# A planner's numbers changed in a float32 hybrid-attention layer: loads' consumers listed later behind their transfers, equal slack for float32 steps

## The chip, the cores and the metric

The kernel runs on one core of a Trainium2 chip. The core has five engines that run side by side, each through its own list of instructions in order: TensorE (PE, matmuls and transposes), VectorE (DVE), ScalarE (ACT), GpSimd (POOL) and SyncE (SP), which here issues nearly all transfers between the chip's memory (DRAM) and the core's buffers. An instruction that waits holds everything listed behind it on its engine. The metric is the device time of one execution in microseconds (us); of several runs the median is given.

## The reference

One layer over 2048 tokens of width 1024, all in float32:

```python
xn = rms_norm(x, mix_norm_g)
aq, ak, av, mq, mk, mv, mo, ipre, fpre, ga, gm = split(xn @ w_in)
att = chunk_band_attention(aq, ak, av, rel_bias)        # 8 heads of 64, own chunk of 64 tokens and 8 before
mq, mk = split(silu(causal_depthwise_conv([mq, mk])))
hm = rms_norm_per_head(mlstm_chunkwise(mq, mk, mv, ipre, fpre))   # 4 heads of 128, chunkwise recurrence
y = sigmoid(ga) * (att @ w_att_proj) + sigmoid(gm) * (sigmoid(mo) * hm @ w_mlstm_proj)
x = x + y @ w_out
x = x + square(relu(rms_norm(x, ffn_norm_g) @ w_up)) @ w_down     # inner width 4096
return rms_norm(x, final_norm_g)
```

## The kernel before, in words

The tokens are four blocks of 512; a tile is 128 partitions by 512 columns. A float32 product is made of three faster ones in the format float32r: each operand is split into a high part (rounded on ACT, a `copy` into float32r) and a low part (`tensor_sub` on DVE, the operand minus its high part), and `mm3` adds high*high, high*low and low*high in a PSUM bank. Such pairs of parts lie in the tiles `r` (activations) and `wsp` (weights). Matmuls of this kind are L631, L662, L667, L562 to L564 and L856 in the profile.

The large products use a seven-product scheme on 2 x 2 blocks instead of eight products. So sums and differences of blocks are formed on DVE (L1765, L1855, L520, L438), spilled to DRAM by `store` (L2043), and loaded back later. The stages follow each other: the first input projections (`quad`, L631), the far ones (`in_far`, `product`, L662 and L667) with the token mixers of blocks 0 and 1 between them, the output projection and the up projection of blocks 0 and 1, their down projection (`down`, L562 to L564) with the mixers of blocks 2 and 3 between, and the same again for blocks 2 and 3. The mixers are attention (`scores` L1337, `turn` L1369, `weigh` L1262) and recurrence (`rec_head`, L1586 to L1651).

What sets the order is a planner, `Flow`, that runs on the host when the kernel is built. Every piece of work is a generator ("thread") that yields an engine and an expected time, for example `yield "act", act_ns(512)`; for a transfer, `yield "sp", 800, 2000` says that the queue is held for 800 ns and the data are there 2000 ns after that. The planner keeps a clock for each engine and always takes the thread whose step can start first. Nothing of this is executed on the chip: the times only decide in what order instructions are listed; what an instruction waits for on the chip are semaphores. Behind the planner the framework's own list scheduler may still move instructions within some microseconds of plan time.

Three of the planner's rules matter here.

- A step on PE gets extra time before it counts as ready: `FAR` for float32r work, `SLACK` for a step that works in full float32 and so switches PE over (marked `"pe~"`: transposes L1369, L1651, L1586, the recurrence's products L1597, L1612 to L1616), and `NEAR` when PE is already in full float32.
- `fl.put(pool, tile, late=...)` gives a tile back to its pool as of a later time, so that its next writer is listed later.
- A load's third number is how long behind its queue time the consumer is listed. `take_u1` (L2101) loads a spilled operand into an `r` tile and then rounds it, L1109 on ACT and L1114 on DVE; it serves the far input projections (from `xu`), the mixers' results (from `mix`) and the down projections (from `u`). `square_kept` (L2070) loads a tile to square it (L2075, L2079). The gate load in `rec_head` is L1648.

`store` (L2042) yields the queue, issues the transfer, sets its event at once and gives the tile back to its pool. `kept_row` (L1715) loads such a spilled tile again; its rounding, with a factor, is L1111 on ACT and L1116 on DVE. L780 is the evacuation of a bank in `park_v` and `finish_far`; L501 and L503 split a weight tile.

Loads into operand tiles go through a ring: 16 tiles in the far projections and in the second down projection, 8 in the first one (`N_RING = (8, 16)`). The tiles named below are `r` (operand parts), `wsp` and `wraw` (split and raw weights), `tmp`, `ctx` (512-column scratch), `sc` (scores), `bank` (PSUM).

Of the kernel before, what the change touches and what calls it, by code (L numbers as in the profile page):

```python
# [101 lines left out]
class Flow:  # L102
# [3 lines left out]

    SLACK, FAR = 720.0, 1300.0
    NEAR = 150.0  # L110
    SWITCH = 85.0
    LAT = dict(pe=dict(act=190.0, dve=190.0, pool=190.0),
# [2 lines left out]
               sp=dict())  # L115
# [114 lines left out]
def act_ns(n, ps=False, ap=0):  # L230
    return (51 if ps else 93) + 0.834 * n + 93 * ap


def dve_ns(n):
    return 70 + 1.042 * n
# [10 lines left out]


class Layer:
    LATE = 4000.0

    def __init__(self, tc, pool, psum, io):
        self.tc, self.nc, self.io = tc, tc.nc, io
# [197 lines left out]
    def split_w(self, i, src, raw, sent=None):  # L450
        if i == 0:
            yield from self.split_first(src, raw, sent)
            self.fl.put(self.wraw, raw, late=self.LATE)
            return
# [4 lines left out]
        yield from self.split_now(i, raw)  # L459
        self.fl.put(self.wraw, raw, late=self.LATE)  # L460

    def split_turned(self, i, srcs, raw):
# [3 lines left out]
        yield from self.split_now(i, raw)  # L466
        self.fl.put(self.wraw, raw, late=self.LATE)

# [38 lines left out]
    def quad_w(self, i, q, kept, raws, evs):  # L507
# [10 lines left out]
        def sub(n, dst, x, y):  # L518
            yield "dve", dve_ns(1024)
            V.tensor_sub(dst, x, y)  # L520
            if kept:
                fl.spawn(keep(n, dst), 1)
            else:
                fl.set(spilt[n])
# [16 lines left out]
        yield from sub(2, b, d, b)  # L541
        fl.put(self.wraw, d, late=self.LATE)
        yield "wait", [spilt[1]]
        yield from sub(3, a, c, a)
        fl.put(self.wraw, c, late=self.LATE)
        yield from self.split_now(i + 5, b)
        yield "wait", [spilt[2]]
        fl.put(self.wraw, b, late=self.LATE)
        yield from self.split_now(i + 6, a)
# [1020 lines left out]
    def rec_head(self, b, h, r):  # L1570
# [72 lines left out]
        fl.put(self.hs, hs)  # L1643
        (og,) = yield "get", self.temp, 1
        yield "wait", [self.m_ev[b, 2 * MH + h]]
        yield "sp", 800, 2000
        nc.sync.dma_start(og[:, :512], self.mfar[b].ap()[2 * MH + h])
        (bk,) = yield "get", self.banks, 1  # L1648
        yield "pe~", 107 * NT
# [391 lines left out]
    def store(self, dst, src, ev, pool=None, item=None, queue="sp"):  # L2041
        yield queue, 800, 2000  # L2042
        self.nc.sync.dma_start(dst, src)  # L2043
        self.fl.set(ev)
        if pool is not None:
            self.fl.put(pool, item)

    def norm_mid(self, s, h):

# [19 lines left out]

    def square_kept(self, src, j, x, tot, summed, scale=1.0):  # L2070
        x5 = x[0][:, :512]
        yield "sp", 800, 2000
        self.nc.sync.dma_start(x5, src)
        yield "act", act_ns(512)
        self.nc.scalar.activation(tot if j == 0 else x5, x5, AF.Square, scale=scale)  # L2075
        if j > 0:
            yield "wait", [summed[j - 1]]
            yield "dve", dve_ns(512)
            self.nc.vector.tensor_add(tot, tot, x5)  # L2079
        self.fl.put(self.sc, x)  # L2080
        self.fl.set(summed[j])
# [17 lines left out]
        fl.put(self.rpool, *(yield "get", ring, N_RING[s]))  # L2099

    def take_u1(self, src, r, ev):  # L2101
        yield "sp", 800, 2000
        self.nc.sync.dma_start(r[:, 1].bitcast(F32), src)
        yield from self.split(r[:, 1].bitcast(F32), r)
        self.fl.set(ev)
# [458 lines left out]
```

## Time and profile before

| what | value |
|---|---|
| runs shown | 2749.84, 2750.84 and 2754.76 us, median 2750.84 |
| profiled execution, its own time | 2753.07 us |
| its span, first to last instruction | 2751.3 us |
| granted TensorE clock | 0.998 |
| busy share of the span | PE 99%, weight loads 82%, DVE 76%, ACT 55%, POOL 2% |
| transfers | 673.57 MB, 244 GB/s over the span |

A page of the profile gives busy time by engine and by group of instructions. The timeline gives instructions in order of time: start, duration, engine, line, operation, tiles written and read, and in brackets how long the engine had been idle before and what ended that. The list of waits sums this idle time by who waited for whom: total, number of times, longest. A matmul's end is modelled in the trace, so a matmul's row is longer than the distance to the next one.

### The profile page before, as it was taken

Reading aid. Unit: us, or ns where it says so; the run is one execution under the profiler, and the core shown is the slowest. Engines: PE = TensorE matmul, PEld = TensorE weight load, DVE = VectorE, ACT = ScalarE, POOL = GpSimd, SP = SyncE. Lnnn points to the kernel's source line nnn. Section 1 sums busy time; section 2 is a strip of 40 time slices with the busy share of each in tenths; the row PEclk is TensorE's granted clock in tenths of the full one; section 3 lists DMA queues with packets and bytes.
Section 4 is the critical chain, followed back from the end, with each engine's and each line's share of the span. In section 5 each row is a group of like instructions: output and inputs, shape, how many; then the busy total and the mean of one; then the engine's idle time right before and its main releaser. Section 6 shows DMA issues by size and latency. Waiting matters only on the chain.

```text
span 2751.3 us, 38074 instructions
## 1 busy us (share of the span) xinstructions
PE 2724.6 (99%) x12832; PEld 2261.5 (82%) x12832; DVE 2086.0 (76%) x3689; ACT 1526.4 (55%) x2640; POOL 44.6 (2%) x79
## 2 busy tenths in 40 slices
PE   9999999999999999999999999999999999999998
PEld 8878888788888887888888888888888888888887
DVE  7878776888775778897768889888888665667675
ACT  6545446666652434566556766657345565554443
POOL 0000000000000000000000000000000000000000
PEclk9999999999999999999999999999999999999999
DMA  8877678878877888767668778776864454588863
GB/s 295 284 254 268 234 267 281 260 235 266 255 256 254 299 305 294 244 212 260 246 237 295 254 231 223 239 257 199 294 227 171 151 205 154 180 278 281 283 230 137
DMA packets 331992, 673.57 MB, mean 245 GB/s; under 512 B 36900, under 2 KB 66468, under 8 KB 331796
## 3 DMA queue, kind: packets, MB, share of 16 engines
q1 hardware_dynamic: 331076, 670.08, 72.3%
q8 instruction: 101, 1.65, 0.2%
q10 hardware_dynamic: 720, 1.06, 0.1%
q14 instruction: 95, 0.78, 0.1%
HBM read 458.79 MB, written 212.21 MB: 244 GB/s over the span
## 4 chain that ended last, share of the span: by engine, by line
PE 83%; DVE 7%; DMA 4%; issue 3%; ACT 2%; POOL 0%; SPq 0%; POOLq 0%; DVEq 0%; ACTq 0%
PE bank L631 35%; PE bank L662 9%; PE bank L562 9%; PE bank L564 8%; PE bank L563 8%; PE bank L667 2%; PE bank L1337 2%; PE bank L1262 2%; PE bank L1369 2%; DVE wsp L503 1%; PE bank L856 1%; DVE r L1114 1%; DMA yp<-tmp 1%; DMA r<-u 1%; DVE ctx L1765 1%
## 5 line engine op out<-in xcount | busy, mean ns | idle before, releaser
L631 PE MATMUL bank<-r,wsp 128*128 128x512 f32 x4872 | 1110.9, 390 | 4.2 <-ACT r L1109 1.4
L631 PEld LDWEIGHTS bank<-r,wsp 128*128 128x128 f32 x4872 | 912.5, 188 | 198.2 <-ACT r L1109 2.1
L501 ACT CAST wsp<-wraw 128x1024 fp32r<-128x1024 f32 x439 | 461.3, 1051 | 492.1 <-PE bank L631 183.3
L503 DVE TENSOR_TENSOR wsp<-wraw,wsp 128x1024 fp32r<-128x1024 f32 x439 | 537.0, 1223 | 247.0 <-ACT wsp L501 236.7
L562 PE MATMUL bank<-r,wsp 128*128 128x512 f32 x1088 | 429.9, 396 | 0.3 <-DVE scs L1343 0.3
L564 PE MATMUL bank<-r,wsp 128*128 128x512 f32 x1088 | 425.3, 391 | 0.0
L563 PE MATMUL bank<-r,wsp 128*128 128x512 f32 x1088 | 425.2, 391 | 0.0
L662 PE MATMUL bank<-r,wsp 128*128 128x512 f32 x1512 | 370.8, 394 | 3.1 <-DVE ctx L780 2.5
L662 PEld LDWEIGHTS bank<-r,wsp 128*128 128x128 f32 x1512 | 279.4, 189 | 59.4 <-issue 2.7
L564 PEld LDWEIGHTS bank<-r,wsp 128*128 128x128 f32 x1088 | 204.3, 188 | 43.0
L562 PEld LDWEIGHTS bank<-r,wsp 128*128 128x128 f32 x1088 | 204.5, 188 | 38.4 <-DVE scs L1343 0.7
L563 PEld LDWEIGHTS bank<-r,wsp 128*128 128x128 f32 x1088 | 204.7, 188 | 38.1
L1114 DVE TENSOR_TENSOR r<-r 128x512 fp32r<-128x512 f32 x273 | 181.8, 687 | 56.8 <-ACT r L1109 55.0
L1109 ACT CAST r<-r 128x512 fp32r<-128x512 f32 x273 | 164.7, 621 | 104.4 <-DMA r<-u 77.1
L1798 DVE TENSOR_TENSOR ctx<-bank,ctx 128x512 f32<-128x512 f32 x150 | 103.0, 687 | 64.7 <-PE bank L631 63.6
L520 DVE TENSOR_TENSOR wraw<-wraw,wraw 128x1024 f32<-128x1024 f32 x112 | 136.5, 1220 | 2.2 <-DMA wsum<-wraw 1.0
L1350 ACT ACTIVATE sc<-sc,scs 128x640 f32<-128x640 f32 (+4 forms) x128 | 97.2, 760 | 54.9 <-DVE scs L1343 54.3
L1790 ACT COPY ctx<-bank 128x512 f32<-128x512 f32 x150 | 87.2, 581 | 52.0 <-PE bank L631 50.5
L2119 ACT ACTIVATE ctx<-ctx 128x512 f32<-128x512 f32 x96 | 60.5, 630 | 97.8 <-DVE ctx L1798 97.8
L1374 DVE TENSOR_TENSOR r<-bank,r 128x512 fp32r<-128x512 f32 (+1 forms) x168 | 96.4, 595 | 8.4 <-ACT r L1372 7.5
L1262 PE MATMUL bank<-r,r 128*128 128x512 f32 x336 | 95.7, 367 | 3.5 <-DVE ctx L1674 1.9
L1372 ACT CAST r<-bank 128x512 fp32r<-128x512 f32 (+1 forms) x168 | 80.7, 514 | 27.9 <-PE bank L1369 27.4
(257 smaller groups left out, 3054.1 us busy)
## 6 DMA issues: line engine op xcount, KB each, us to landing
wraw<-in_wf SPq DMA_DIRECT2D x196, 512.0 KB, 4.2
r<-u SPq DMA_DIRECT2D x224, 256.0 KB, 4.4
wraw<-wsum SPq DMA_DIRECT2D x104, 512.0 KB, 4.5
u<-ctx SPq DMA_DIRECT2D x128, 256.0 KB, 2.8
u<-tmp SPq DMA_DIRECT2D x96, 256.0 KB, 2.1
wraw<-in_w SPq DMA_DIRECT2D x47, 512.0 KB, 4.5
ctx<-in_wf SPq DMA_DIRECT2D x88, 256.0 KB, 4.2
wsum<-ctx SPq DMA_DIRECT2D x88, 256.0 KB, 3.1
```

Of the source, the lines that this page charges most:

```text
L501: nc.scalar.copy(w[:, 0], raw)
L503: nc.vector.tensor_sub(w[:, 1], raw, w[:, 0].bitcast(F32))
L520: V.tensor_sub(dst, x, y)
L562: mm(ps, lh, rh, start=first, stop=False)
L563: mm(ps, lh, rl, start=False, stop=False)
L564: mm(ps, ll, rh, start=False, stop=last)
L631: mm(ps, wv[:, x, k, n], a[:, y], start=new and k == 0 and x == y == 0, stop=k == 3 and x == 1, skip_group_check=True)
L662: mm(ps, wv[:, x, k, n], a[:, y], start=start and x == y == 0, stop=stop and x == 1, skip_group_check=True)
L1109: self.nc.scalar.copy(dst[:, 0], src)
L1114: self.nc.vector.tensor_sub(dst[:, 1], src, dst[:, 0].bitcast(F32))
L1262: nc.tensor.matmul(bkv[:, :, c0:c0 + w], st, sl[:, :, o:o + w], start=n == 0, stop=n == total - 1)
L1798: nc.vector.tensor_add(t[:, o:o + 512], ps, t[:, o:o + 512])
```

## The change

The change edits seven numbers of the planner; no computation is added or taken away.

```diff
-    SLACK, FAR = 720.0, 1300.0
+    SLACK, FAR = 1300.0, 1300.0
...
-    LATE = 4000.0
+    LATE, LANDED = 4000.0, 10000.0
...
         yield "wait", [self.m_ev[b, 2 * MH + h]]
-        yield "sp", 800, 2000
+        yield "sp", 800, 4500
         nc.sync.dma_start(og[:, :512], self.mfar[b].ap()[2 * MH + h])
...
         if pool is not None:
-            self.fl.put(pool, item)
+            self.fl.put(pool, item, late=1500.0)
...
     def square_kept(self, src, j, x, tot, summed, scale=1.0):
         x5 = x[0][:, :512]
-        yield "sp", 800, 2000
+        yield "sp", 800, 5000
...
     def take_u1(self, src, r, ev):
-        yield "sp", 800, 2000
+        yield "sp", 800, self.LANDED
         self.nc.sync.dma_start(r[:, 1].bitcast(F32), src)
         yield from self.split(r[:, 1].bitcast(F32), r)
```

So the rounding of an operand that `take_u1` loads is listed 10 us instead of 2 us behind its transfer, the squaring 5 us, the gate's use 4.5 us; a tile whose content `store` sends off is given back 1.5 us later; and a float32 step is held back on PE as long as a float32r one. Line numbers stay the same.

Since the planner orders everything by these times, instructions move on every engine. Three places are shown.

First, ACT in the far input projections, where the first operands loaded from `xu` are rounded (L1109, tiles `r20` and those behind it). `L1672` and `L1680` take the recurrence's products out of their banks, L1273 the attention's, L1372 the transposed scores, L739 an input projection's bank. Before:

```order
L1930 ACTIVATE ctx10_123<-bank2_131 128x512
L739 COPY ctx5_118<-bank4_133 128x512
L1372 COPY r0_68<-bank1_130 128x512
L1109 COPY r20_88<-r20_88 128x512
L1672 ACTIVATE ctx2_115<-bank5_134,g_ex_175 128x129
L1372 COPY r5_73<-bank3_132 128x512
L1273 COPY tmp2_109<-bank7_136 64x512
L1680 ACTIVATE tmp5_112,hs0_176<-ctx2_115 128x128
```

And of the change:

```order
L1372 COPY r10_78<-bank4_133 128x256
L1672 ACTIVATE ctx5_118<-bank6_135,g_ex_175 128x129
L1680 ACTIVATE tmp3_110,hs1_177<-ctx5_118 128x128
L1672 ACTIVATE ctx5_118<-bank7_136,g_ex_175 128x129
L1680 ACTIVATE tmp5_112,hs1_177<-ctx5_118 128x128
L1109 COPY r20_88<-r20_88 128x512
L1109 COPY r25_93<-r25_93 128x512
L1109 COPY r16_84<-r16_84 128x512
L1109 COPY r18_86<-r18_86 128x512
```

The first rounding stood ahead of the evacuations L1672, L1372 and L1273 of that moment; now four roundings stand together behind two more rounds of the recurrence's L1672 and L1680.

Second, DVE at the end of the projections of blocks 0 and 1, where the merged tiles `yp` are loaded back into `tmp` and rounded (L1116); L992 merges a gate with a bank. Before:

```order
L1116 TENSOR_SCALAR r23_91<-tmp1_108,r23_91 128x512
L1116 TENSOR_SCALAR r2_70<-tmp5_112,r2_70 128x512
L503 TENSOR_TENSOR wsp2_63<-wraw0_64,wsp2_63 128x1024
L1116 TENSOR_SCALAR r7_75<-tmp2_109,r7_75 128x512
L1116 TENSOR_SCALAR r12_80<-tmp3_110,r12_80 128x512
L780 TENSOR_TENSOR ctx9_122<-bank0_129,ctx9_122 128x512
L992 TENSOR_SCALAR tmp0_107<-tmp0_107,bank4_133 128x512
```

And of the change:

```order
L1116 TENSOR_SCALAR r2_70<-tmp3_110,r2_70 128x512
L503 TENSOR_TENSOR wsp2_63<-wraw0_64,wsp2_63 128x1024
L1116 TENSOR_SCALAR r7_75<-tmp2_109,r7_75 128x512
L1116 TENSOR_SCALAR r12_80<-tmp5_112,r12_80 128x512
L780 TENSOR_TENSOR ctx7_120<-bank1_130,ctx7_120 128x512
L1116 TENSOR_SCALAR r4_72<-tmp3_110,r4_72 128x512
L1116 TENSOR_SCALAR r9_77<-ctx10_123,r9_77 128x512
```

The operand whose load stands last in SP's list (`r2` from `tmp5` before, `r4` from `tmp3` now) was second of four and stood ahead of the evacuation L780; now it stands behind L780. SP's list at this place, before (L984 loads a gate for the merge, L456 a weight tile):

```order
L2043 DMA yp1<-tmp5_112 128x512
L1715 DMA ctx14_127<-yp1 128x512
L1715 DMA tmp5_112<-yp0 128x512
L456 DMA wraw3_67<-wsum26 128x1024
L984 DMA tmp1_108<-gate1 128x512
```

And of the change:

```order
L2043 DMA yp1<-tmp4_111 128x512
L1715 DMA ctx0_113<-yp1 128x512
L984 DMA tmp4_111<-gate1 128x512
L456 DMA wraw3_67<-wsum26 128x1024
L1715 DMA tmp3_110<-yp0 128x512
```

The second row behind the store wrote to the tile that was being stored (`tmp5`) and was an operand's load; the row that now writes to a tile just stored (`tmp4`) is a gate's load, and the operand's load follows two rows later.

Third, ACT near the start of the first down projection, where operands from `u` are rounded between the weight splits (L501) and the mixers of blocks 2 and 3 (L1350, L1357 scale scores; L1285, L1273, L1672, L1680 as above). Before:

```order
L1350 ACTIVATE sc2_103,scs2_104<-sc2_103,scs2_104 128x640
L501 COPY wsp1_62<-wraw1_65 128x1024
L1285 COPY r19_87<-tmp5_112 64x256
L1109 COPY r27_95<-r27_95 128x512
L1109 COPY r13_81<-r13_81 128x512
L1372 COPY r23_91<-bank5_134 128x512
L1109 COPY r26_94<-r26_94 128x512
L1372 COPY r24_92<-bank2_131 128x256
L1109 COPY r6_74<-r6_74 128x512
L501 COPY wsp2_63<-wraw2_66 128x1024
```

And of the change:

```order
L1590 ACTIVATE ctx4_117<-bank5_134,g_ex_175 128x128 x4
L1273 COPY tmp5_112<-bank2_131 64x512
L501 COPY wsp2_63<-wraw2_66 128x1024
L1109 COPY r9_77<-r9_77 128x512
L1109 COPY r13_81<-r13_81 128x512
L1672 ACTIVATE ctx11_124<-bank1_130,g_ex_175 128x129
L1109 COPY r26_94<-r26_94 128x512
L1350 ACTIVATE sc3_105,scs3_106<-sc3_105,scs3_106 128x640
L1109 COPY r6_74<-r6_74 128x512
```

The four roundings stood ahead of the weight split into `wsp2`; now they stand behind it.

## The prediction

> **What bounds the kernel.** I read the page's first part, then the list of PE's waits, then the timeline around the longest of them, and last the waits of ACT and the landing times of the loads.
>
> ```profile
> span 2751.3 us, 38074 instructions
> PE 2724.6 (99%) x12832; PEld 2261.5 (82%) x12832; DVE 2086.0 (76%) x3689; ACT 1526.4 (55%) x2640; POOL 44.6 (2%) x79
> ```
>
> PE is busy for all but 2751.3 - 2724.6 = 26.7 us, and the change takes no matmul away. So the most that any order of the same work can win is about 1%, while what it can lose has no such bound. Where the idle time lies is in the list of PE's waits (total, times, longest); these are the rows on which I rest something.
>
> ```profile
> PE bank L662 <- DVE ctx L780: 2.5, 2, 2.3
> PE bank L1262 <- DVE ctx L1674: 1.9, 1, 1.9
> PE bank L1369 <- ACT sc L1357: 1.6, 3, 0.8
> PE bank L631 <- ACT r L1109: 1.4, 1, 1.4
> PE bank L1463 <- DVE g_lf L1461: 1.1, 1, 1.1
> PE bank L1262 <- DVE tmp L1275: 1.1, 1, 1.1
> PE bank L631 <- DVE ctx L1798: 1.1, 2, 0.6
> PE bank L1369 <- DVE sc L1355: 1.0, 2, 0.9
> PE bank L1612 <- DVE scs L1352: 0.6, 1, 0.6
> PE bank L1651 <- DVE ctx L1641: 0.6, 1, 0.6
> ```
>
> These ten rows hold 12.9 us in 15 waits, 0.9 us each; no wait is long. A wait costs a little more than its row, since a matmul's modelled end reaches past the start of the next one:
>
> ```profile
> 1050.33 5.60 PE L662 MATMUL bank<-r,wsp 128*128 128x512 f32 x24
> L662 PE MATMUL bank<-r,wsp 128*128 128x512 f32 x1512 | 370.8, 394 | 3.1 <-DVE ctx L780 2.5
> ```
>
> 24 matmuls take 5.60 us from the first start to the last end, and one row is 0.394 us long (the mean of the group): (5.60 - 0.39)/23 = 0.227 us from start to start. So 0.394 - 0.227 = 0.16 us of each wait are hidden in the row before it, and a wait that goes wholly gives that back too.
>
> **Part by part. Roundings listed 10 us behind (LANDED).** Three of the waits start with an ACT that is held at a rounding L1109 whose load has not landed. The first:
>
> ```profile
> 744.30 0.62 ACT L1109 CAST r<-r 128x512 fp32r<-128x512 f32 x1 [4.46 <-DMA r<-xu]
> 744.82 0.36 ACT L1672 ACTIVATE ctx<-bank,g_ex 128x129 f32<-128x129 f32 x1
> 745.56 0.29 DVE L1674 TENSOR_TENSOR ctx<-bank,ctx 128x129 f32<-128x129 f32 x1
> 745.90 1.04 PE L1262 MATMUL bank<-r,r 128*128 128x512 f32 x2 [1.89 <-DVE ctx L1674]
> ```
>
> ACT is idle 4.46 us, the evacuation L1672 queued behind it starts 0.5 us after, DVE's L1674 follows, and PE gets its bank 1.89 us late. In the new list L1672 stands ahead of the roundings. The second and the third:
>
> ```profile
> 1603.60 0.62 ACT L1109 CAST r<-r 128x512 fp32r<-128x512 f32 x1 [1.69 <-DMA r<-u]
> 1606.46 0.69 DVE L1275 TENSOR_TENSOR tmp<-bank,tmp 64x512 f32<-64x512 f32 x1
> 1607.21 0.50 PE L1262 MATMUL bank<-r,r 128*128 128x512 f32 x1 [1.09 <-DVE tmp L1275]
> 1712.61 0.62 ACT L1109 CAST r<-r 128x512 fp32r<-128x512 f32 x1 [0.58 <-DMA r<-u]
> 1713.26 0.69 DVE L1114 TENSOR_TENSOR r<-r 128x512 fp32r<-128x512 f32 x1 [0.16 <-ACT r L1109]
> 1714.30 0.40 PE L1463 MATMUL bank<-g_lf,const 128*128 128x16 f32 x2 [1.13 <-DVE g_lf L1461]
> ```
>
> At 1607 the hold of 1.69 us is longer than PE's wait, so all 1.09 us go. At 1714 the gate chain on DVE (L1457, L1461) stands behind L1114: without it DVE would be 0.69 + 0.16 = 0.85 us earlier, out of 1.13. Together 1.89 + 1.09 + 0.85 = 3.8 us. The bounds: 0 if the held time only goes to another evacuation, 4.1 if everything goes.
>
> ```profile
> ACT r L1109 <- DMA r<-u: 77.1, 64, 3.9
> DMA to landing us min/median/max: 2.6/4.4/8.2
> ```
>
> The second row is of these loads (L2103, from `u`, `xu` and `mix`). 10 us behind the queue's time covers the longest, 8.2; 2 us covered none. So nearly all of the 77.1 us of holds on ACT vanish, but only those three places are seen by PE: in the down projections PE is fed far ahead, and ACT is busy 55% of the time. On the Trainium skill: "DMA: Bandwidth & Descriptors", section "Anatomy of one DMA", puts a transfer on the path it describes at about 2.0 us fixed plus its bytes at 436 GB/s, an estimate of 2.6 us for these 256 KB. It speaks against this part, since listing at 2 us would then be 0.6 us short at most and three holds would give back 1.8 us instead of 3.8, a median 2.0 us above the one forecast below; the trace agrees with it for the quickest load only, and the measured median, 4.4, decides.
>
> **Stored tiles back 1.5 us later.** The longest wait of all is at 1058 us:
>
> ```profile
> 1045.23 0.42 SPq L2043 DMA_DIRECT2D yp<-tmp  x1
> 1050.89 0.32 SPq L1715 DMA_DIRECT2D tmp<-yp  x1
> 1053.47 0.63 ACT L1111 ACTIVATE r<-tmp 128x512 fp32r<-128x512 f32 x1 [7.02 <-DMA tmp<-yp]
> 1054.13 0.69 DVE L1116 SCALAR_TENSOR_TENSOR r<-tmp,r 128x512 fp32r<-128x512 f32 x1 [6.35 <-ACT r L1111]
> 1057.42 0.68 DVE L780 TENSOR_TENSOR ctx<-bank,ctx 128x512 f32<-128x512 f32 x1
> 1058.25 2.09 PE L662 MATMUL bank<-r,wsp 128*128 128x512 f32 x8 [2.32 <-DVE ctx L780]
> ```
>
> SP holds the load of the second operand until the store out of the same tile has landed, 1050.89 - 1045.23 = 5.7 us, with weight and gate loads queued behind it; ACT is held 7.02 us, DVE 6.35, and the evacuation L780 behind them frees PE's bank 2.32 us late. 1.5 us is far less than 5.7, so SP is held again, now at a gate's load into `tmp4`, and the last operand's load goes out after two more rows, near 1051.7. But in the new list L780 stands ahead of that operand's rounding on DVE, so the bank is freed before. What is late next is the operand: loaded by about 1051.7 + 2.6 = 1054.3 (2.6 as from 1050.89 to 1053.47), rounded by 1055.6, ahead of the second L780, which is wanted a tile of 12 matmuls (2.7 us) after the first. I take the whole 2.3; the bounds are 0 (the second L780 waits instead) and 2.3.
>
> **Equal slack for float32 steps.** A transpose or a recurrence product that opens a float32 stretch is listed 1300 - 720 = 580 ns of plan time later, so what it waits for is ahead of it by that much more, and float32r products of the same stage cover PE. Of the rows above these are the longest one of L1355 (0.9), L1612 and L1651 (0.6 each): 3 x 0.58 = 1.7 us. The three waits L1369 <- L1357 lie inside a float32 stretch, where another number (NEAR) holds, and stay. Bounds: 0 and 2.1.
>
> **Squares and gates.** L631 <- L1798 has one wait of 0.6 (near 2231 us) behind a held L2075, whose loads need 3.5 us in the median:
>
> ```profile
> DMA to landing us min/median/max: 2.6/3.5/6.4
> ```
>
> 5 us instead of 2 covers the median: 0.5 us, between 0 and 0.6. PE waits nowhere for the gate's multiplication (L1653), so the 4.5 us there cost and bring nothing on PE; ACT and DVE have the room.
>
> **What it adds.** Near the start of the first down projection the four roundings now stand behind the weight split L501 instead of ahead of it.
>
> ```profile
> L501 ACT CAST wsp<-wraw 128x1024 fp32r<-128x1024 f32 x439 | 461.3, 1051 | 492.1 <-PE bank L631 183.3
> L503 DVE TENSOR_TENSOR wsp<-wraw,wsp 128x1024 fp32r<-128x1024 f32 x439 | 537.0, 1223 | 247.0 <-ACT wsp L501 236.7
> ```
>
> The split waits for the last matmuls on the old weight tile. From there it takes 1.05 us on ACT, then 1.22 on DVE (L503), and only then the first operand's low part, 0.69 (L1114 above): 3.0 us. In the new list 5 matmuls of 0.227 and about 7 shorter products of 0.2 stand on PE between, 2.6 us: 0.4 us of new wait, between 0 and 1.5 if the three roundings behind are late as well. And every engine's list is redrawn, so waits arise where there were none. Counted in the lists, PE rows that have less than 2 us of matmuls between them and the last PE result that their releaser's queue needs fall from 69 to 30, and those with less than 9 us when a transfer lies in between from 49 to 5, so I allow few: three new ones, one for each class of loads moved, at 0.7 us, 2.1 us; between 0 and the 9 us of a dozen.
>
> **The sum.** 3.8 + 2.3 + 1.7 + 0.5 = 8.3, and 0.16 for each of six waits that go wholly, 1.0: 9.3 us. Less 0.4 and 2.1: 6.8 us. Against the profiled execution, 2753.07 us (the span and 1.8 us around it), that gives 2746.3; the median of the runs, 2750.84, lies 2.2 below the profiled one, so the median after should be 2744.0 us.
>
> **The rivals.** *The waits form anew elsewhere.* The named waits go, but the 15 waits above are a sample of what any such list leaves; with new ones worth 6 us instead of 2 the median is 2748. For it speaks that no wait is longer than 2.4 us and that the lists are redrawn from the first stage on; against it, the two counts above. *The roundings become late (the slower case).* In the first down projection the ring has 8 tiles, two groups of four; a group lasts 48 matmuls, 48 x 0.227 = 10.9 us. Listed 10 us behind its transfer, a rounding has little left of those 10.9 us, and if ACT's list puts evacuations and weight splits between, PE waits once a group. There are 7 x 4 = 28 groups: at 0.7 us each 19.6 us, less the gain of 6.8, +12.8 us, 2764. It decides from (6.8 + 5.5)/28 = 0.44 us a group upwards. Against it: loads land 4.4 us after issue, and at the third place shown I count only 0.4, once. *The change does little:* SP still waits for landed stores, as shown, and if L780 is held again as well, 2.5 us stay: 2746.5.
>
> **How the numbers follow.** What a measurement of this kernel can tell from no change is about 0.2%, 5.5 us: below 2745.3 is faster, above 2756.3 slower. My forecast, with its gain between 5.5 and 15 us: 0.57. Waits anew, or L780 held again, within 5.5 us: 0.29. Late roundings or more new waits than a dozen: 0.14. The likeliest case alone spans 2736 to 2745; with the second case the range goes to 2756, and leaves out the slower case and the few per cent in which nearly all of PE's waits vanish.
>
> **What would show it.** In the changed profile: the row L1109 <- DMA r<-u on ACT falls from 77 us to below 10; no PE wait on L1674, L1275 or L1461 that starts with a held L1109; none of 2.3 us on L780; PE's idle time falls from 26.7 to about 20 us. If PE waits often on L1109 or L1114 between 1520 and 1800 us, the slower rival holds. The prediction falls if the redrawn lists bring a wait of several microseconds at a place I haven't looked at, for instance where a stage begins.

## The result and the profile after

| what | before | after |
|---|---|---|
| median of six runs each | 2751.21 us | 2737.49 us |
| lowest and highest | 2749.84, 2754.76 | 2734.73, 2738.84 |
| profiled execution, its span, its granted clock | 2753.07, 2751.3, 0.998 | 2734.73, 2732.9, 1.000 |

The ratio is 0.9947, with a 95% interval of 0.9937 to 0.9957: 13.7 us or 0.5% faster. The forecast was 6.8 us. The profiled execution after is the fastest of its six, so the two profiles lie 18.3 us apart, 4.6 more than the medians.

The page of the changed kernel, its first part:

```profile
span 2732.9 us, 38055 instructions
PE 2717.4 (99%) x12832; PEld 2262.6 (83%) x12832; DVE 2074.9 (76%) x3685; ACT 1527.6 (56%) x2650; POOL 48.2 (2%) x79
```

The matmuls are the same 12832. PE's idle time is now 2732.9 - 2717.4 = 15.5 us instead of 26.7. The list of PE's waits of the changed kernel is complete in these rows (total, times, longest):

```profile
PE bank L563 <- DVE r L1287: 1.6, 1, 1.6
PE bank L631 <- ACT r L1109: 1.1, 1, 1.1
PE bank L1068 <- POOL r_in L1033: 1.0, 1, 1.0
PE bank L304 <- DVE ones L299: 0.9, 1, 0.9
PE bank L662 <- DVE ctx L755: 0.8, 1, 0.8
PE bank L1369 <- ACT sc L1357: 0.6, 2, 0.4
PE bank L662 <- DVE r L1374: 0.5, 1, 0.5
PE bank L631 <- DVE r L1114: 0.4, 1, 0.4
PE bank L1337 <- DVE scs L1343: 0.4, 1, 0.4
PE bank L631 <- DVE r L1116: 0.3, 1, 0.3
PE bank L1369 <- DVE scs L1343: 0.2, 1, 0.2
```

They add up to 7.8 us in 12 waits. The same list of the kernel before adds up to 18.8 us in 27. So 11.0 us of recorded waits are gone, and 15 waits fewer at the prediction's 0.16 us each make 2.4 more: 13.4 us, near the 13.7 of the medians. The two profiled executions from which these rows come lie 18.3 us apart, though; what else they hold is told in the last section. The three waits of the first 480 us (L631, L1068, L304, 3.0 us) belong to the start and hardly changed; behind them 15.4 us in 24 waits became 4.8 us in 9.

None of the rows names L1674, L1275, L1461 or L780, the four on which the prediction put 6.1 us. At the first of those places, ACT's timeline of the changed kernel reads:

```profile
736.40 0.31 ACT L1680 ACTIVATE tmp<-ctx 128x128 f32<-128x128 f32 x1 [0.36 <-DVE ctx L1674]
736.71 2.17 ACT L1109 CAST r<-r 128x512 fp32r<-128x512 f32 x4
738.78 0.83 ACT L1350 ACTIVATE sc<-sc,scs 128x640 f32<-128x640 f32 x1
```

Four roundings run one behind the other and have no bracket: their loads have landed. At the second place, the merged tiles, ACT's and DVE's rows are:

```profile
1046.07 0.68 DVE L780 TENSOR_TENSOR ctx<-bank,ctx 128x512 f32<-128x512 f32 x1
1046.72 0.63 ACT L1111 ACTIVATE r<-tmp 128x512 fp32r<-128x512 f32 x1 [1.98 <-DMA tmp<-yp]
1047.39 0.69 DVE L1116 SCALAR_TENSOR_TENSOR r<-tmp,r 128x512 fp32r<-128x512 f32 x1 [0.63 <-ACT r L1111]
1049.19 0.68 DVE L780 TENSOR_TENSOR ctx<-bank,ctx 128x512 f32<-128x512 f32 x1
```

ACT still waits for a merged tile, but 1.98 us instead of 7.02, and DVE's L780 runs at 1046.07, ahead of L1116, the part of the rounding that depends on that tile; PE has no wait there. ACT's own list of waits, all of whose rows for the loads of `take_u1` in the changed kernel are

```profile
ACT r L1109 <- DMA r<-u: 27.6, 30, 3.5
ACT r L1109 <- DMA r<-xu: 2.8, 2, 2.4
ACT r L1109 <- DMA r<-mix: 0.3, 1, 0.3
```

shows fewer holds at L1109: 27.6 us in 30 for the down projections, down from 77.1 in 64.

### The profile page after: what moved, and what is told of

It reads as the page before. It is cut to its first block, busy times and chain, and to the rows that moved or that the text cites. A ratio compares the mean times of both kernels' runs of the same rounds, so it can differ in the third digit from the quotient of the medians.

```text
span 2732.9 us, 38055 instructions
## 1 busy us (share of the span) xinstructions
PE 2717.4 (99%) x12832; PEld 2262.6 (83%) x12832; DVE 2074.9 (76%) x3685; ACT 1527.6 (56%) x2650; POOL 48.2 (2%) x79
## 4 chain that ended last, share of the span: by engine, by line
PE 90%; DVE 6%; issue 1%; DMA 1%; ACT 1%; POOL 0%; SPq 0%; POOLq 0%; DVEq 0%; ACTq 0%
PE bank L631 37%; PE bank L662 11%; PE bank L562 9%; PE bank L563 9%; PE bank L564 9%; PE bank L667 3%; PE bank L1337 2%; PE bank L1262 2%; PE bank L1369 2%; PE bank L856 1%; DVE wsp L503 1%; DVE r L1114 1%; DMA x<-ctx 1%; PE bank L1420 1%; PE bank L1597 1%
## 5 line engine op out<-in xcount | busy, mean ns | idle before, releaser
L631 PE MATMUL bank<-r,wsp 128*128 128x512 f32 x4872 | 1110.6, 390 | 1.9 <-ACT r L1109 1.1
L631 PEld LDWEIGHTS bank<-r,wsp 128*128 128x128 f32 x4872 | 912.6, 188 | 194.9 <-ACT r L1109 1.8
L501 ACT CAST wsp<-wraw 128x1024 fp32r<-128x1024 f32 x439 | 461.3, 1051 | 540.9 <-PE bank L563 203.7
L563 PE MATMUL bank<-r,wsp 128*128 128x512 f32 x1088 | 425.0, 391 | 1.6 <-DVE r L1287 1.6
L662 PE MATMUL bank<-r,wsp 128*128 128x512 f32 x1512 | 368.5, 393 | 1.3 <-DVE ctx L755 0.8
L662 PEld LDWEIGHTS bank<-r,wsp 128*128 128x128 f32 x1512 | 278.9, 188 | 58.3 <-DVE ctx L755 1.5
L563 PEld LDWEIGHTS bank<-r,wsp 128*128 128x128 f32 x1088 | 204.6, 188 | 40.4 <-DVE r L1287 2.0
L1114 DVE TENSOR_TENSOR r<-r 128x512 fp32r<-128x512 f32 x271 | 179.8, 688 | 16.1 <-ACT r L1109 13.4
L1109 ACT CAST r<-r 128x512 fp32r<-128x512 f32 x271 | 157.9, 617 | 31.0 <-DMA r<-u 27.6
L1798 DVE TENSOR_TENSOR ctx<-bank,ctx 128x512 f32<-128x512 f32 x150 | 103.0, 687 | 64.1 <-PE bank L631 64.0
L520 DVE TENSOR_TENSOR wraw<-wraw,wraw 128x1024 f32<-128x1024 f32 x112 | 136.2, 1219 | 3.8 <-DMA wsum<-wraw 2.8
L1350 ACT ACTIVATE sc<-sc,scs 128x640 f32<-128x640 f32 (+4 forms) x128 | 97.5, 762 | 67.1 <-DVE scs L1343 66.4
L1374 DVE TENSOR_TENSOR r<-bank,r 128x512 fp32r<-128x512 f32 (+1 forms) x168 | 95.6, 593 | 14.5 <-ACT r L1372 13.8
L1372 ACT CAST r<-bank 128x512 fp32r<-128x512 f32 (+1 forms) x168 | 80.9, 515 | 31.3 <-PE bank L1369 29.3
```

Of the source, the lines that this page charges most:

```text
L501: nc.scalar.copy(w[:, 0], raw)
L563: mm(ps, lh, rl, start=False, stop=False)
L631: mm(ps, wv[:, x, k, n], a[:, y], start=new and k == 0 and x == y == 0, stop=k == 3 and x == 1, skip_group_check=True)
L662: mm(ps, wv[:, x, k, n], a[:, y], start=start and x == y == 0, stop=stop and x == 1, skip_group_check=True)
L1109: self.nc.scalar.copy(dst[:, 0], src)
L1114: self.nc.vector.tensor_sub(dst[:, 1], src, dst[:, 0].bitcast(F32))
```

## The experiments

Each kernel below computes the whole layer and is timed against runs of the kernel before on the same chip; the ratio is to those runs, with its 95% interval. Edits are shown against the kernel that each expectation starts from. The change sets five numbers (the slack and those of `take_u1`, the gate, the squares and the stored tiles); the gate and the squares are tried together, so there are four edits.

**Slack alone.**

```diff
-    SLACK, FAR = 720.0, 1300.0
+    SLACK, FAR = 1300.0, 1300.0
```

> The kernel before with SLACK = 1300 alone; the loads' and the stores' numbers stay. Theory A (each edit takes away its own class of waits, and the effects add): the waits that open a float32 stretch shrink by 0.58 us each, so the time falls by 1.7 to 4 us, ratio 0.9985 to 0.9994; the three waits behind held roundings (L1674, L1275, L1461) and the 2.3 us on L780 stay. Theory B (any redrawn list moves the time by several us, whichever number redraws it): anything between -8 and +8 us, with other waits than before.

Measured: 1.0008 (0.9998 to 1.0018). The slack alone gains nothing, against the 1.7 to 4 us of theory A. PE's recorded waits rise from 18.8 us in 27 to 23.6 in 36.

**Later roundings alone (LANDED).**

```diff
+    LATE, LANDED = 4000.0, 10000.0
...
     def take_u1(self, src, r, ev):
-        yield "sp", 800, 2000
+        yield "sp", 800, self.LANDED
```

> The kernel before with LANDED = 10000 in take_u1 alone. Theory A: the 77 us of ACT's holds at L1109 fall below 30, the three PE waits behind them go, 3.8 to 5 us in all, ratio 0.998 to 0.9986; the 2.3 us on L780 stay. Theory B: anything between -8 and +8 us.

Measured: 0.9973 (0.9963 to 0.9983), 7.4 us, about half of the whole gain and more than theory A expected, with waits of 14.3 us in 21. It is the only one of the four edits that gains alone.

**Stored tiles back later, alone.**

```diff
-            self.fl.put(pool, item)
+            self.fl.put(pool, item, late=1500.0)
```

> The kernel before with late=1500 in store alone. Theory A: PE's 2.3 us on L780 near 1058 us go and nothing else, 2 to 2.5 us, ratio 0.9991 to 0.9993; ACT's holds at L1109 stay near 77 us. Theory B: anything between -8 and +8 us.

Measured: 1.0019 (1.0010 to 1.0027), slower, where theory A expected a gain. The 2.3 us wait on L780 at 1058 us is gone, but another on the same line has taken its place, and the wait on L1674 is longer than before. PE's timeline and the first row of its list of waits:

```profile
1102.27 3.00 PE L662 MATMUL bank<-r,wsp 128*128 128x512 f32 x12 [1.96 <-DVE ctx L780]
```

```profile
PE bank L1262 <- DVE ctx L1674: 2.4, 1, 2.4
```

**Squares and gates alone.**

```diff
         yield "wait", [self.m_ev[b, 2 * MH + h]]
-        yield "sp", 800, 2000
+        yield "sp", 800, 4500
...
     def square_kept(self, src, j, x, tot, summed, scale=1.0):
-        yield "sp", 800, 2000
+        yield "sp", 800, 5000
```

> The kernel before with 5000 in square_kept and 4500 at the recurrence's gate load alone. Theory A: one wait of PE on L1798 goes, 0.5 us, ratio 0.9995 to 1.0; holds of ACT at L2075 behind sc<-x fall. Theory B: anything between -8 and +8 us.

Measured: 1.0006 (0.9995 to 1.0016), no gain, waits of 16.4 us in 30. The four ratios multiplied give 1.0006; the change itself gives 0.9947. So the theory that each edit removes its own waits and that the effects add has fallen.

**The change without the slack.**

```diff
-    SLACK, FAR = 1300.0, 1300.0
+    SLACK, FAR = 720.0, 1300.0
```

> The changed kernel with SLACK back at 720. The edits alone gave 1.0008 (slack), 0.9973 (LANDED), 1.0019 (stores) and 1.0006 (squares and gates), together 0.9947, so they do not add: product of the four 1.0006. Theory C (the slack works only once ACT and DVE are no longer held by late loads): without it the ratio goes back to 0.9965 to 0.998, and PE waits again for L1355, L1357 and L1612 by 3 us and more in all. Theory D (LANDED does it all, the rest is the luck of the list): 0.994 to 0.996 as with it.

Measured: 0.9963 (0.9949 to 0.9977), waits of 12.5 us in 21. Next to 0.9947 the slack, which gains nothing by itself, is worth about 0.16%, 4.4 us, within the whole. The intervals overlap, but beside the kernel of the second blank below, whose runs were made on the same chip as these, the two sets of runs lie apart: 2744.2 to 2747.1 us without the slack, 2737.5 to 2741.8 with it. The ratio lies between the two expected ranges, and the waits on L1355, L1357 and L1612 hold 2.5 us, not 3.

**The change without the stored tiles' delay.**

```diff
-            self.fl.put(pool, item, late=1500.0)
+            self.fl.put(pool, item)
```

> The changed kernel with stored tiles back at once. Theory C (stores matter beside the others): the wait on L780 near 1058 us is back, ratio 0.9955 to 0.9965. Theory D (luck of the list): 0.992 to 0.998, the wait on L780 not back. Alone the edit gave 1.0019.

Measured: 0.9942 (0.9927 to 0.9957). The delay is worth nothing in the whole either, and the wait of 2.3 us is not back without it: at its place PE waits 0.6 us. Three of the four edits carry the gain.

**Two blanks.** A number that should not matter is moved by 10 ns of plan time, which redraws the lists from the first stage on: once in the kernel before, once in the changed one.

```diff
-    NEAR = 150.0
+    NEAR = 160.0
```

> A blank: the kernel before with NEAR = 160 instead of 150, a number that none of the edits touches and whose 10 ns should buy nothing; it redraws the lists only. It measures what a redrawn list alone is worth. If the edits' own effects are real beyond luck: within 0.9990 to 1.0010 (3 us). If the luck of a redrawn list is as large as the effects alone: up to 0.997 or 1.003.

> The same blank on the changed kernel. If the changed kernel's 0.9947 is owed to its numbers: 0.9937 to 0.9960. If it was a lucky draw: 0.996 to 0.999, nearer to the kernel with LANDED alone, 0.9973.

Measured: 0.9998 (0.9986 to 1.0011) from the kernel before, and 0.9943 (0.9927 to 0.9958) from the changed one against the kernel before. Both redrawn kernels stay where they were, within 0.04%. Single waits do change: in the redrawn kernel before, the wait of 2.3 us on L780 at 1058 us is gone with none of the edits made, and the one on L1674 has grown to 2.7 us; but the sum stays, 17.6 us in 26. So the gain isn't the luck of one drawing. Each kernel was redrawn once, and the kernels with part of the edits were not.

**Later roundings and slack together.**

```diff
-    SLACK, FAR = 720.0, 1300.0
+    SLACK, FAR = 1300.0, 1300.0
...
+    LATE, LANDED = 4000.0, 10000.0
...
-        yield "sp", 800, 2000
+        yield "sp", 800, self.LANDED
```

> The kernel before with LANDED = 10000 and SLACK = 1300, nothing else. Theory C (the slack pays once the roundings no longer hold ACT; squares, gates and stores are worth nothing): 0.9940 to 0.9955, as the whole change. Theory E (the loads of squares and gates must be covered too before the slack pays): 0.9960 to 0.9975, as LANDED alone.

Measured: 0.9998 (0.9988 to 1.0008), outside both expected ranges. Put on top of the later roundings, the slack takes away what they gained alone. ACT's list of waits shows that the holds went nevertheless:

```profile
ACT r L1109 <- DMA r<-u: 38.9, 29, 4.8
```

Two theories have fallen: that the later roundings do it all, and that the slack pays as soon as roundings no longer hold ACT. With squares and gates added to this kernel (the change without the stored tiles' delay, above) the ratio goes to 0.9942. These loads were the smallest term of the prediction. (The change without squares and gates alone was not run; this kernel lacks the stored tiles' delay too.)

Where the difference lies can be seen in part. PE's waits between 480 and 660 us, the first mixers, are in the kernel with later roundings and slack:

```profile
PE bank L667 <- DVE tmp L1275: 1.8, 2, 1.2
PE bank L1369 <- DVE sc L1355: 1.7, 2, 1.4
PE bank L1586 <- DMA r<-mfar: 0.9, 1, 0.9
```

And the whole of that stretch in the change without the stored tiles' delay, which differs from it by the gate's and the squares' loads alone:

```profile
PE bank L1369 <- ACT sc L1357: 0.6, 2, 0.4
PE bank L662 <- DVE r L1374: 0.5, 1, 0.5
PE bank L1586 <- DMA r<-mfar: 0.3, 1, 0.3
```

The first kernel's total there is 4.8 us, the second's 1.4. The slack alone also has 4.8, the kernel before 3.2. By the planner's rule only the gate's number can act in this stretch, since in these two kernels the first load to be squared goes out at 1117.9 and 1116.6 us. Over all runs, slack without a later gate has 4.8 us there twice; with both numbers five kernels have 1.1 to 1.5 us and one, the kernel with roundings half as late, 3.5; the others, without the slack, 2.8 to 3.2. So slack without a later gate makes waits among the first mixers, and with it at most 1.5 us are left in five kernels of six.

The squares show in one place, the last stage, in the kernel with later roundings and slack:

```profile
2568.88 0.63 ACT L2075 ACTIVATE sc<-sc 128x512 f32<-128x512 f32 x1 [4.02 <-DMA sc<-mid]
2569.54 0.69 DVE L2079 TENSOR_TENSOR sc<-sc,sc 128x512 f32<-128x512 f32 x1 [3.33 <-ACT sc L2075]
2570.29 1.05 PE L2384 MATMUL bank<-ones,sc 128*128 128x2 f32 x8 [2.11 <-DVE sc L2079]
```

A squaring whose load hasn't landed holds ACT 4.02 us, DVE 3.33 and PE 2.11, and PE's clock is halved behind it, 1.7 us more (told in the last section). The kernel with later roundings alone has this wait too, 1.4 us; none of the eight kernels with the squares' later number has it, nor have the four that lack both numbers.

The two profiled executions lie 12.5 us apart. The lists of waits differ by 8.2 us (20.3 and 12.1) and 5 waits, 0.8 at 0.16 each; the clock cost the first kernel 5.1 us and the second 1.7. Together that is 12.4 us. Of it the first mixers hold 3.4 us of waits, and the squaring 2.1 and 1.7 of clock; most of the rest lies between 1480 and 1740 us (5.9 us of waits against 1.7, and the other 3.4 of the first kernel's clock), and why is not shown.

**The change without the later roundings.**

```diff
     def take_u1(self, src, r, ev):
-        yield "sp", 800, self.LANDED
+        yield "sp", 800, 2000
```

> The changed kernel with take_u1 at 2000 again: slack, stores, squares and gates stay. Theory C: ACT's holds at L1109 are back near 80 us, ratio 0.9990 to 1.0015, as those edits alone. Theory F (the edits help each other whatever LANDED is): 0.9970 to 0.9985.

Measured: 0.9971 (0.9960 to 0.9982), 8 us faster than before. ACT's row:

```profile
ACT r L1109 <- DMA r<-u: 82.8, 73, 4.3
```

ACT is held longer than in the kernel before, the gain of 0.29% is there all the same, as theory F expected, and PE has no wait on L1674, L1275 or L1461. With the run before it this shows that the sum of ACT's holds doesn't set the time: 38.9 us of holds and no gain there, 82.8 us and 0.29% here. Next to 0.9947, the later roundings are worth 0.24% in the whole, 6.6 us.

**Roundings listed half as late.**

```diff
-    LATE, LANDED = 4000.0, 10000.0
+    LATE, LANDED = 4000.0, 5000.0
```

> The changed kernel with LANDED = 5000, above the loads' median of 4.4 us and below their longest, 8.2. If it is enough to cover the usual load: 0.994 to 0.996, ACT's holds at L1109 below 40 us. If the late loads are what PE sees, as at 745 us in the kernel before: 0.996 to 0.998, holds of 40 to 60 us.

Measured: 0.9971 (0.9960 to 0.9981), the same as with 2 us and in the second expected range. ACT's row:

```profile
ACT r L1109 <- DMA r<-u: 59.9, 64, 2.7
```

There are as many holds as before the change, only shorter. The estimate that the prediction took from the Trainium skill ("DMA: Bandwidth & Descriptors", section "Anatomy of one DMA") was 2.6 us for such a load on the path that the page describes; by it 5 us would leave no hold. The trace differs: 64 holds of up to 2.7 us behind a listing at 5 us. The plan's 5 us count from the planner's queue time, so lateness of SP itself is in these holds too.

**More slack and more distance.**

```diff
-    SLACK, FAR = 1300.0, 1300.0
+    SLACK, FAR = 1900.0, 1900.0
```

> The changed kernel with SLACK = FAR = 1900. PE's remaining waits before L1374, L755, L1357 and L1343 are 0.2 to 0.8 us each, so 0.6 us more of lead would take 2 to 4 us: 0.9930 to 0.9940. If the lead is already long enough, or tiles and banks are held longer for it: 0.994 to 0.998.

Measured: 1.0010 (1.0001 to 1.0019), outside both expected ranges. The whole gain is gone, though the holds at L1109 are no more than in the changed kernel (26.8 us from `u`). PE's waits between 1740 and 2060 us, the last mixers, first rows:

```profile
PE bank L1262 <- DVE r L1374: 5.4, 3, 2.6
PE bank L1369 <- ACT sc L1357: 1.9, 1, 1.9
PE bank L1337 <- DVE ctx L2183: 1.3, 1, 1.3
```

This stretch holds 11.2 us of the kernel's 20.1; in the changed kernel it holds 1.8. The longest wait in the timelines of DVE and PE:

```profile
1943.17 1.88 DVE L1114 TENSOR_TENSOR r<-r 128x512 fp32r<-128x512 f32 x3
1944.97 0.41 DVE L1280 TENSOR_TENSOR tmp<-tmp 64x256 f32<-64x256 f32 x1
1945.30 0.68 DVE L1374 TENSOR_TENSOR r<-bank,r 128x512 fp32r<-128x512 f32 x1
1946.04 0.78 PE L1262 MATMUL bank<-r,r 128*128 128x512 f32 x2 [2.61 <-DVE r L1374]
```

Three low parts of operands (L1114), 1.88 us, stand ahead of the L1374 for which PE waits. DVE's rows have no bracket: it isn't held there, it is busy with work listed ahead.

The sums of PE's recorded waits by stage, worked out from its list of waits in each stretch (us, with the number of waits):

| kernel | ratio | 0 to 480 | 480 to 660 | 660 to 820 | 820 to 1480 | 1480 to 1740 | 1740 to 2060 | rest |
|---|---|---|---|---|---|---|---|---|
| before | 1 | 3.4/3 | 3.2/7 | 1.9/1 | 4.8/6 | 4.1/7 | 0.9/2 | 0.5/1 |
| the change | 0.9947 | 3.0/3 | 1.1/3 | 0.8/1 | 0.7/2 | 0.4/1 | 1.8/2 | 0 |
| slack alone | 1.0008 | 3.5/4 | 4.8/7 | 1.7/3 | 2.8/3 | 5.6/8 | 3.2/9 | 2.0/2 |
| later roundings alone | 0.9973 | 2.6/3 | 3.2/8 | 1.2/1 | 3.0/4 | 1.0/2 | 0 | 3.3/3 |
| squares and gates alone | 1.0006 | 3.8/5 | 2.9/6 | 1.6/5 | 1.2/3 | 1.3/4 | 2.1/4 | 3.5/3 |
| later roundings and slack | 0.9998 | 2.6/4 | 4.8/7 | 1.7/2 | 1.6/3 | 5.9/5 | 0.2/1 | 3.6/2 |
| without the slack | 0.9963 | 4.3/4 | 3.0/6 | 2.1/4 | 1.5/3 | 0.7/2 | 0.4/1 | 0.5/1 |
| without the later roundings | 0.9971 | 3.2/3 | 1.5/4 | 0.5/1 | 2.4/5 | 2.2/3 | 3.9/4 | 0.6/1 |
| without the stored tiles' delay | 0.9942 | 3.0/5 | 1.4/4 | 2.9/2 | 1.0/2 | 1.7/2 | 1.3/3 | 0.8/1 |
| roundings half as late | 0.9971 | 4.2/5 | 3.5/6 | 0 | 3.0/4 | 3.1/4 | 1.3/1 | 0.5/1 |
| more slack and distance | 1.0010 | 3.4/5 | 1.3/2 | 0 | 2.8/4 | 0.5/2 | 11.2/9 | 0.9/1 |

Over the profiled executions of all 14 kernels, the sum of PE's recorded waits, with 0.16 us more for each, goes with the execution's time at a correlation of 0.95. (These waits are a part of that time, so this says where the time goes, not why.) No kernel is measurably faster than the change: 0.9942 and 0.9943 lie within its interval.

## Why the prediction was right, and where it was wrong

The direction, the range and the bound came out: PE is busy 99%, and what an order can win lies in PE's own list of waits. The size was off, 6.8 us against 13.7, and the way there only partly as told. That the time still fell into the range, 1.5 us above its lower end, is in part luck: no edit's price came out both alone and in the whole.

- **The step that failed is the last of the sum: the named waits go, the others stay, three new ones come.** The prediction left 18.8 - 8.3 = 10.5 us of recorded waits standing and added 2.5. Measured were 7.8 in all. Behind the first 480 us, where the start's waits stay, the named waits (9.0 us in 8 by their rows) are gone, as said. New ones came, rows that the list before doesn't have (L563, L662 on L755 and on L1374, L1337 on L1343): 3.3 us in 4, a little more than forecast. But the others, 6.4 us in 16, did not stay: rows of the same lines hold 1.5 us in 5. These 4.9 us are most of what the sum missed in the waits. In the profile before, the clock behind one named wait was 1.7 more, which the sum didn't have at all.
- **Later roundings, 3.8 us:** measured 7.4 alone and 6.6 in the whole. The three named waits are gone, but they are gone as well without this edit: in the kernel with 82.8 us of holds, and in the kernels with the slack alone and with squares and gates alone, which gain nothing. The price was the right order of size; the reason, that ACT's hold is passed on at three places, isn't what sets it.
- **Stored tiles back later, 2.3 us:** the hold of ACT at L1111 follows the edit, 4.8 to 7.0 us at this place in the seven kernels without it and 0.7 to 3.0 in the seven with it. The wait of PE doesn't: of the seven without it only the kernel before has 2.32 us there, four others 0.3 to 0.8 and two none. So the wait that the prediction priced was one drawing's luck. With the edit there is none at this place, but in six of the seven one of 0.4 to 2.0 us on the same line some 45 us later; only the changed kernel lacks that one too. Alone the edit costs 0.19% (1.0019), and in the whole it is worth nothing.
- **Slack, 1.7 us:** alone nothing (1.0008), with the later roundings a loss of 0.25% (0.9973 to 0.9998), in the whole a gain of about 4.4 us. No single price fits.
- **Squares and gates, 0.5 us:** right alone within the measurement, and far too small in the whole: on top of later roundings and slack they bring 0.9998 to 0.9942. The wait that it priced was misread: near 2231 us it is 0.48 us, and what stands ahead of L1798 on DVE there is L520, 1.22 us of work without a hold; kernels with the squares' later number still have it (0.82 us without the stored tiles' delay). The wait that does begin with a held load of a square is the one on L2079 shown above, which the list before doesn't have. The prediction looked for a PE wait on the gate's L1653, found none and put the gate at nothing. With slack but without the later gate such a wait does stand in PE's list, 1.1 us in the kernel with later roundings and slack, and another of 0.2 among the first mixers.
- **What it adds:** no wait on the weight splits or the operands of the first down projection stands in the list of the changed kernel between 1480 and 1740 us but one of 0.4 us. The slower rival, late roundings at 0.44 us a group, is refuted for this kernel. In the kernel with more slack and distance, L1114 ahead of the mixers' work does delay PE, in another stage.
- **The other rivals:** neither took place. Waits did not form anew to 6 us (3.3 us, above); and L780 was not held again in the changed kernel.
- **The signs to look for:** the holds at L1109 fell to 27.6 us, not below 10; no wait on L1674, L1275 or L1461, none of 2.3 on L780, as said; PE's idle time fell to 15.5 us, not 20.

That the combination is worth more than its parts is shown by the runs. Why is shown in part: slack and gate at the first mixers, with one exception, and the squares at one wait of the last stage. How the rest of the way from 0.9998 to 0.9942 divides between the gate's and the squares' loads stays open, since the two were never run apart. Open too is how much of 0.9998, and of the 1.0010 with more slack, belongs to that one drawing: both kernels were drawn once, and both lost 5.1 us of clock behind a few waits.

## What to carry to other kernels

When one engine is busy 99% of the time, the sum of its own recorded waits is what an order can still win, and it follows the time better than the holds of any engine off the path: 82.8 us of holds on ACT went with a gain, 38.9 with none. Numbers that feed one planner are to be tried together, and each left out once from the best set (here the squares and gates were not left out alone), since four edits that alone give 1.0008, 0.9973, 1.0019 and 1.0006 gave 0.9947 together; a blank move of a number that shouldn't matter tells how much of a gain is luck. More lead isn't always better: 1.9 us instead of 1.3 lost it all, in the one drawing tried. A wait of a single row is a poor thing to price: a blank took the longest one away and left the sum.

## What the runs showed of the hardware

A wait of PE can cost more than its own length. Windows of the kernel before around its wait of 1.89 us at 745.9 us (columns: stretch, length, busy time and instructions of PE, PEld, DVE, ACT and POOL, then PE's granted clock, the DMA share, GB/s):

```profile
742.00:744.00 2.00, 2.00 (x15) 1.63 (x13) 0.14 (x1) 0.00 (x0) 0.00 (x0) 1.00 0.96 370
744.00:746.00 2.00, 0.11 (x2) 0.10 (x1) 1.05 (x3) 1.68 (x4) 0.00 (x0) 1.00 0.61 192
746.00:748.00 2.00, 2.00 (x5) 1.53 (x6) 1.62 (x4) 1.98 (x5) 0.00 (x0) 0.53 0.27 49
748.00:750.00 2.00, 2.00 (x10) 1.69 (x9) 1.84 (x3) 1.69 (x5) 0.00 (x0) 0.61 0.34 119
750.00:752.00 2.00, 2.00 (x12) 1.68 (x11) 1.90 (x5) 0.88 (x2) 0.00 (x0) 1.00 0.79 260
```

Behind the wait the granted clock is 0.53 and 0.61 in two windows: (1 - 0.53) x 2 + (1 - 0.61) x 2 = 1.7 us lost, nearly as much as the wait. At half clock that is a stretch of some 3.5 us. The prediction priced this wait at 1.89. The changed kernel has neither the wait nor the loss (clock 1.00 from 730 to 760 us). The wait of 2.32 us at 1058 us cost no clock (1.00 from 1050 to 1070), so the length of a wait doesn't decide alone. At the place of the first wait, the kernel with the stored tiles' delay alone waits 2.41 us and loses 1.7 of clock, and the blank of the kernel before waits 2.68 us and loses none. The kernel with more slack and distance lost more where its waits are thick:

```profile
1930.00:1940.00 10.00, 5.81 (x28) 4.39 (x27) 9.94 (x24) 7.65 (x14) 0.00 (x0) 0.82 0.65 219
1940.00:1950.00 10.00, 7.39 (x30) 6.89 (x30) 10.00 (x27) 4.22 (x11) 0.00 (x0) 0.67 0.43 131
```

That is (0.18 + 0.33) x 10 = 5.1 us, and its 11 runs have a mean granted clock of 0.9968, beside 0.9987 for the kernel before. With that its profile adds up: 12.3 us more of recorded waits than the changed kernel, 11 waits at 0.16 (1.8) and 5.1 of clock are 19.2; the two profiled executions lie 18.9 apart. The kernel with later roundings and slack also lost 5.1 us of clock, 1.7 in each of three places, behind waits of 2.00, 1.50 and 2.11 us. Between before and after the same sum is 11.0 + 2.4 + 1.7 = 15.1 of 18.3; 3.2 us stay unexplained.

The Trainium skill, "TensorE: Matmul & The Clock Gate", section "Part 1: The HAM clock gate", has the clock halved after an idle window of about 3.4 us that runs freely, and back after as long a busy one. The trace agrees on the half and on the 3.5 us of its duration; it differs on the cause, since here 1.89 us without a matmul were enough once, and 2.32 us were not another time.
